# Six projections in one closing chain of Strassen products, in a hybrid decoder layer on one core

## The chip, the core and the metric

The kernel runs on one core of one Trainium2 chip. A core has a matrix engine (PE, with its weight loads listed apart as PEld), a vector engine (DVE), a scalar engine (ACT), GpSimd (POOL) and a queue engine (SP) that issues every DMA of this kernel. The metric is the device time of one execution in microseconds (us), lower is better. The kernel before takes 2838.16 us, the median of 3 runs from 2836.1 to 2838.73.

## The reference

One decoder layer over 512 tokens of width 2048: sliding-window attention with sinks, a gated DeltaNet branch, and a gated merge of the two. Everything is float32. Cut to what the change touches:

```python
proj = h @ w_in                      # 512 x 2048 times 2048 x 21056
aq, ak, av, ag, d_qkv, dz, db, da, mg_a, mg_b = split(proj)
a_out = swa_attention(rope(norm(aq)), rope(norm(ak)), av, sinks) * silu(ag)
y_a = a_out @ w_o_swa                # 2048 x 2048
o = gated_delta_rule(q, k, v, g, beta)          # 32 heads, 128 wide
o = rms_norm(o, dn_norm_w) * silu(dz)           # dz: the output gate, 4096 wide
y_b = o @ w_o_dn                     # 4096 x 2048
y = sigmoid(mg_a) * y_a + sigmoid(mg_b) * y_b   # mg_a, mg_b: the merge gates, 2048 wide each
return x + gate * (y @ w_out)        # 2048 x 2048
```

## The kernel before, in words

**Products.** Each float32 operand is cut into a high part (`hi`, fp32r) and a rest (`lo`); `split` does it with a cast on ACT (L61) and a subtraction on DVE (L62). `mm3` then issues three matmuls of 128x512 (L273, L274, L275: high by high, high by low, low by high). A *channel tile* (`channel_tile`) makes 128 channels for all 512 tokens: 16 steps of 128 along the contraction, so 48 matmuls, with the weights stationary and the token matrix `hh`/`hl` moving. Its weights are one load of 1 MB (`raw`, L215), split in two halves of 1024 columns. There are 174 channel tiles. The other way is a Strassen product (the Winograd form, `PRODUCTS`): tokens, contraction and columns are each cut in two, seven products of sums take the place of eight of quarters, and per 2048x2048 matrix there are 2 column parts x 7 = 14 products of 48 matmuls, where channel tiles need 16 x 48. In a product the token form is stationary and the weights move; a half of 1024 columns feeds 12 matmuls per product step instead of 24. Four of the seven products use sums of weight quarters. `weight_sums` forms these ahead: for one matrix 8 blocks, each with four loads of 512 KB (L1241), four additions of 128x1024 on DVE (L1246) and four stores (L1248).

**Stages.** `startup` (norm, adaLN, first tiles), `delta_keys` (16 key tiles for DeltaNet, with merge-gate tiles `mb` between them), `attention` (2 key, 16 query and 16 gate tiles, then seven merge-gate tiles `ma`), `delta_heads` (16 groups of two heads; each has the tiles q, v, v, z, z and a chain `scan` over four chunks of 128 tokens), `branch_b` (the two halves of `w_o_dn`, by Strassen, 28 products), `finish` (16 channel tiles `os` for `w_o_swa`, merged with the gates) and `output` (`w_out`, by Strassen, 14 products).

**What sets the order.** Work between matmuls is written as generators; `pump` is called once in 6 matmuls and steps them. `go` starts one that counts its waits in pumps, `paced` one that costs a budget per pump (the triangular `solve_all` at 0.36, `weight_sums` at 2.0), and `behind` ties an instruction after the latest matmul. A scheduler then fixes one order per engine; each engine and the SP queue run theirs in order. Weight loads take turns in two buffers (`wraw`), split halves in three (`whl`), so DVE can be at most three halves ahead of PE.

The steps that the prediction names: in `scan`, `pp` (L971) gives `r` on DVE (L974), then `pv` (L981), `vn` on ACT (L983), `vs` on DVE (L988), `pod` (L996 to L1000), `osb` and its squares on ACT (L1001, L1004), the new state `S` on DVE (L1011); after the last chunk a reciprocal root (`rsqrt`), the scaling of `osb` (L1030), a transposition `pto` and a product with the gate (L1037).

## Time and profile before

| | |
|---|---|
| median of 3 runs | 2838.16 us |
| the profiled execution, its span | 2839.0 us |
| PE busy | 2806.5 us (99%), 14152 matmul records |
| DVE busy | 1944.8 us (69%) |
| ACT busy | 1207.1 us (43%) |
| moved by DMA | 603.25 MB, mean 212 GB/s, queue q1 at 62.1% of 16 engines |
| vector and scalar work on one weight half | 1235 ns (L62) and 1050 ns (L61), 516 times |

A page of the profile gives busy time per engine, 40 slices of the span with the busy share in tenths, the DMA queues, the chain of waits followed back from the end, and groups of instructions by line with their mean and what ended the idle time before them. Matmuls overlap in the records, so their mean duration is longer than their spacing. The profiled execution's span is 0.8 us over the median of the runs; nothing lies around it that the runs would add.

### The profile page before, as it was taken

The numbers are of one execution on the slowest core, as the hardware profiler recorded it, in microseconds if no ns is written. First come the engines' busy times: TensorE is split into PE (matmuls) and PEld (weight loads), VectorE is DVE, ScalarE is ACT, GpSimd is POOL, SyncE is SP. The second block draws the span as 40 slices with busy tenths as digits, with TensorE's granted clock in tenths as the row PEclk, the third lists the DMA queues.
The fourth block names the chain that finished last, engine by engine and source line by source line (L and its number), as shares of the span: only waits on it lengthen the run. The fifth ranks groups of instructions, "written<-read, shape, count | busy, mean of one in ns | idle before, by whom it ended". The sixth has DMA issues, their size and how long they took to land.

```text
span 2839.0 us, 38354 instructions
## 1 busy us (share of the span) xinstructions
PE 2806.5 (99%) x14152; PEld 2283.3 (80%) x14152; DVE 1944.8 (69%) x3185; ACT 1207.1 (43%) x2476; POOL 146.0 (5%) x124
## 2 busy tenths in 40 slices
PE   8999999999999999999999999999999999999999
...
DVE  7866876867758667778766666666656766664676
...
GB/s 402 335 246 230 257 218 139 110 91 91 82 135 119 101 168 110 117 201 219 247 255 262 235 224 242 210 239 238 231 167 252 289 314 240 302 273 180 242 318 168
DMA packets 228512, 603.25 MB, mean 212 GB/s; under 512 B 76354, under 2 KB 102594, under 8 KB 188002
## 3 DMA queue, kind: packets, MB, share of 16 engines
q1 hardware_dynamic: 228324, 600.80, 62.1%
...
## 4 chain that ended last, share of the span: by engine, by line
PE 91%; DMA 3%; DVE 3%; ACT 1%; issue 1%; SPq 0%; POOL 0%; DVEq 0%; ACTq 0%; POOLq 0%
PE mm L273 22%; PE mm L275 21%; PE mm L274 21%; PE m L274 5%; PE m L273 5%; PE m L275 5%; PE pod L1000 1%; PE O L1514 1%; PE pv L981 1%; DVE wlo L62 1%; PE pod L999 1%; PE pod L996 1%; PE pp L971 1%; PE S L1451 1%; DMA wa<-in_w_ada_ss 1%
## 5 line engine op out<-in xcount | busy, mean ns | idle before, releaser
L273 PE MATMUL mm<-hh,whi 128*128 128x512 f32 x2784 | 1130.4, 406 | 1.5 <-ACT hh L61 1.5
L275 PE MATMUL mm<-hh,wlo 128*128 128x512 f32 x2784 | 1090.4, 392 | 0.0
L274 PE MATMUL mm<-hl,whi 128*128 128x512 f32 x2784 | 1087.9, 391 | 0.0
L62 DVE TENSOR_TENSOR wlo<-raw,whi 128x1024 fp32r<-128x1024 f32 x516 | 636.9, 1235 | 426.4 <-ACT whi L61 415.4
L61 ACT CAST whi<-raw 128x1024 fp32r<-128x1024 f32 x516 | 541.3, 1050 | 799.9 <-PE mm L274 566.6
L273 PEld LDWEIGHTS mm<-hh,whi 128*128 128x128 f32 x2784 | 524.0, 188 | 117.0 <-issue 14.3
L275 PEld LDWEIGHTS mm<-hh,wlo 128*128 128x128 f32 x2784 | 523.0, 188 | 113.8 <-issue 0.2
L274 PEld LDWEIGHTS mm<-hl,whi 128*128 128x128 f32 x2784 | 524.7, 188 | 100.9 <-issue 1.6
L1246 DVE TENSOR_TENSOR q<-q,q 128x1024 f32<-128x1024 f32 x96 | 124.8, 1300 | 0.0
L794 ACT ACTIVATE E<-E,neg_g 128x128 f32<-128x128 f32 x256 | 81.2, 393 | 92.3 <-POOL E L788 89.6
L831 DVE TENSOR_TENSOR A<-A,atmp 128x62 f32<-128x62 f32 (+30 forms) x124 | 109.5, 883 | 0.6
L823 DVE TENSOR_TENSOR atmp<-A 128x62 f32<-128x62 f32 (+30 forms) x124 | 107.4, 866 | 0.4
L928 POOL TENSOR_TENSOR qe<-qe,yq 128x512 f32<-128x512 f32 x32 | 54.1, 1708 | 923.9 <-DMA qe<-eg_rows 695.9
L1001 ACT COPY osb<-pod 128x256 f32<-128x256 f32 x64 | 23.8, 372 | 152.6 <-PE pod L1000 152.6
L788 POOL TENSOR_SCALAR_AFFINE_SELECT E<-E 128x512 f32<-128x512 f32 x64 | 59.1, 936 | 431.2 <-DMA E<-g_rows 384.5
L983 ACT COPY vn<-pv 128x256 f32<-128x256 f32 x64 | 23.8, 372 | 124.4 <-PE pv L981 124.4
L652 DVE SCALAR_TENSOR_TENSOR yv<-mm,convh,yv 128x511 f32<-128x511 f32 (+2 forms) x96 | 71.2, 742 | 1.1
L988 DVE TENSOR_SCALAR vs<-vn,kd 128x128 f32<-128x128 f32 x96 | 23.1, 283 | 58.3 <-ACT vn L983 58.3
L1482 ACT ACTIVATE sm<-sm,mx,rs 128x128 f32<-128x128 f32 x128 | 61.5, 482 | 3.4 <-DVE mx L1477 2.3
L1011 DVE SCALAR_TENSOR_TENSOR S<-S,egl,pod 128x128 f32<-128x128 f32 x64 | 19.3, 342 | 51.0 <-ACT junk L1004 51.0
L472 DVE SCALAR_TENSOR_TENSOR wa<-wa,silu_cb 128x2048 f32<-128x2048 f32 x22 | 50.1, 2285 | 4.8 <-DMA wa<-in_w_ada_ss 4.8
L657 ACT ACTIVATE th<-yv 128x512 f32<-128x512 f32 x32 | 20.1, 630 | 76.4 <-DVE yv L652 73.7
...
## 6 DMA issues: line engine op xcount, KB each, us to landing
...
```

The lines of the kernel that those rows point to most:

```text
L61: h = self.nc.scalar.copy(out=hi, in_=src)
L62: l = self.nc.vector.tensor_tensor(out=lo, in0=src, in1=hi.bitcast(F32), op=ALU.subtract)
L273: nc.tensor.matmul(ps, lhsT=wh, rhs=xh, start=first, stop=False)
L274: nc.tensor.matmul(ps, lhsT=wh, rhs=xl, start=False, stop=False)
L275: self.last_mm = nc.tensor.matmul(ps, lhsT=wl, rhs=xh, start=False, stop=last)
L652: nc.vector.scalar_tensor_tensor(out=y[:, s:], in0=ps[:, : T - s], scalar=w[:, j : j + 1], in1=y[:, s:], op0=ALU.mult, op1=ALU.add)
L788: self.last_mask = self.nc.gpsimd.affine_select(out=E, in_=E, pattern=[[0, NTB], [1, P]], compare_op=ALU.is_ge, fill=NEG, base=0, channel_ ...
L794: self.nc.scalar.activation(E[:, c, :], E[:, c, :], AF.Exp, bias=self.neg_g[:, c, h : h + 1])
L823: eng.tensor_tensor(out=t, in0=A[:, m : m + 1, m + 1 :].to_broadcast([P, m, n]), in1=A[:, :m, m : m + 1].to_broadcast([P, m, n]), op=ALU.mult,
L831: self.behind(eng.tensor_tensor(out=A[:, :m, m + 1 :], in0=A[:, :m, m + 1 :], in1=t, op=ALU.add))
L1246: self.behind(nc.vector.tensor_tensor(out=q[f], in0=q[x], in1=q[y], op=ALU.add))
L1482: nc.scalar.activation(t, t, AF.Exp, scale=r[:, h : h + 1], bias=mx[:, h : h + 1], accum_out=den[:, h : h + 1])
```

## The change

Three more matrices, the two merge gates (`ga`, `gb`) and `w_o_swa` (`os`), are multiplied by Strassen products. They and the two halves of `w_o_dn` (`d0`, `d1`) and `w_out` (`out`) form one chain `tail` of 84 products. The gate products use the token matrix `hh`/`hl` itself for three of their forms and make the other four from it (`h_forms`); the gates are stored by tokens (`gate_t`), so that the merge happens by tokens when a product of `os`, `d0` or `d1` is evicted; `d1`'s results are transposed in PSUM and become the forms of `out` (`out_forms`). Eight gate products come first (`EARLY`), two of them at the end of `delta_heads`.

The channel tiles that stood between keys and in attention, `mb` and `ma`, go. Output-gate tiles `z` take their places: 18 in `delta_keys`, 7 in `attention`, 7 stay in `delta_heads` (`ZHEADS`). A `z` tile is now activated, stored to DRAM (`z_d`) and read back by `scan`, so `heads` has three or four tiles per group instead of five. Weight sums are formed for six matrices instead of three: `ga`'s in `delta_keys`, `gb`'s in `attention` with additions of 128x512, the other four in `delta_heads` from group 0 on (before: from group 3). In `scan`, `vs` moves from DVE to ACT, as does a copy `Y`. The third weight buffer exists for the whole tail; `out` had five and has three.

By count, PE has 12504 instructions instead of 12792: 288 fewer of 128x512 and nothing else. DVE has 3400 instead of 3163, among them 159 more of 128x1024; ACT 2254 instead of 2081, among them 95 more casts of 128x1024; SP issues 1782 DMAs instead of 1370.

**PE, the last head group and the tail behind it.** `mm` and `m` are the big products, the others the last steps of `scan`. Before:

```order
L981 MATMUL pv<-r,tt_9106 128x128
L981 MATMUL pv<-r,tt_9108 128x128
L273 MATMUL mm<-hh,whi 128x512
...
L999 MATMUL pod<-S,qe 128x128
L1000 MATMUL pod<-vn,E 128x128
L273 MATMUL mm<-hh,whi 128x512
...
L275 MATMUL mm<-hh,wlo 128x512
L320 MATMUL pto<-ident,osb 128x128 x4
```

Between the last `pod` and `pto` 36 big matmuls stand there. With the change:

```order
L957 MATMUL pp<-S,kT 128x256
L266 MATMUL m_17720<-wlo,hh 128x512
L267 MATMUL m_17720<-whi,hl 128x512
L265 MATMUL m_17720<-whi,hh 128x512
L967 MATMUL pv<-r,tt_9523 128x128
...
L984 MATMUL pod<-vn,E 128x128
L265 MATMUL m_17720<-whi,hh 128x512
L266 MATMUL m_17720<-wlo,hh 128x512
L267 MATMUL m_17720<-whi,hl 128x512
L314 MATMUL pto<-ident,osb 128x128 x8
L265 MATMUL m_17721<-whi,hh 128x512
```

Three big matmuls stand between `pp` and `pv`, and three between the last `pod` and `pto`.

**DVE at the start of attention.** `wlo` is the split of a weight half, `kms`, `arky`, `arkt` the reciprocal root of the attention keys, `ang` and `turns` the rotary angles, `atmp` and `A` the solve, `q` a weight sum. Before:

```order
L62 TENSOR_TENSOR wlo<-raw,whi 128x1024
L73 TENSOR_TENSOR arkt<-arkt,kms 128x512
L831 TENSOR_TENSOR A<-A,atmp 128x30x33
L74 SCALAR_TENSOR_TENSOR arky<-arkt,arky 128x512
L72 SCALAR_TENSOR_TENSOR arkt<-arky 128x512
...
L823 TENSOR_TENSOR atmp<-A 128x992
L1367 TENSOR_TENSOR ak<-ak,arky 128x512
L62 TENSOR_TENSOR wlo<-raw,whi 128x1024
```

Eight instructions stand between the two splits. With the change:

```order
L69 TENSOR_TENSOR wlo<-raw,whi 128x1024
L1516 TENSOR_SCALAR ang<-ang 128x512
L1524 TENSOR_SCALAR sin<-sin,sgn 128x512
...
L1612 TENSOR_SCALAR kms<-kss 128x512
L76 TENSOR_SCALAR arky<-kms 128x512
L79 SCALAR_TENSOR_TENSOR arkt<-arky 128x512
L819 TENSOR_TENSOR atmp<-A 128x992
...
L1490 TENSOR_TENSOR q_4988<-q_4988,q_4990 128x512
...
L1540 TENSOR_TENSOR ak<-ak,partner_4683 128x512
L69 TENSOR_TENSOR wlo<-raw,whi 128x1024
```

Now 38 stand between two splits: 8 on the angles, 22 of both key roots, 4 that scale and rotate a key, 3 of the solve and one sum.

**DVE in the first head groups.** Here `r` and `S` are the steps of `scan`, `q` the sums. Before:

```order
L62 TENSOR_TENSOR wlo<-raw,whi 128x1024
L831 TENSOR_TENSOR A<-A,atmp 128x49x14
L1246 TENSOR_TENSOR q_11387<-q_11387,q_11396 128x1024
L1011 SCALAR_TENSOR_TENSOR S<-S,egl,pod 128x128 x2
...
L1246 TENSOR_TENSOR q_11396<-q_11396,q_11398 128x1024
L659 SCALAR_TENSOR_TENSOR yq<-th,yq 128x512
L831 TENSOR_TENSOR A<-A,atmp 128x50x13
L62 TENSOR_TENSOR wlo<-raw,whi 128x1024
```

With the change:

```order
L69 TENSOR_TENSOR wlo<-raw,whi 128x1024
L80 TENSOR_TENSOR rot<-rot,ms 128x8
...
L1490 TENSOR_TENSOR q_10797<-q_10797,q_10799 128x1024
L1490 TENSOR_TENSOR q_10799<-q_10799,q_10801 128x1024
L992 COPY S<-pod 128x256
L1490 TENSOR_TENSOR q_10801<-q_10797,q_10801 128x1024
L819 TENSOR_TENSOR atmp<-A 128x962
L1490 TENSOR_TENSOR q_10823<-q_10801,q_10823 128x1024
L960 SCALAR_TENSOR_TENSOR r<-pp,neg_eg,vt 128x128 x2
L69 TENSOR_TENSOR wlo<-raw,whi 128x1024
```

All four sums of a block, two or one between two splits before, stand between the same two splits, 26 instructions apart, and the next two splits follow each other closely.

The diff, cut to its core (`...` marks what is left out):

```diff
+GEMMS = ["ga", "gb", "os", "d0", "d1", "out"]
+YS = ["s1", "a12", "s2", "a22", "s4"]
+EARLY = [(e, n, m) for e in range(2) for n in range(2) for m in (0, 3)]
+ZKEYS = 18
+ZATT = 7
+ZHEADS = {2 * g + 1 for g in (1, 3, 5, 8, 10, 12, 15)}
+ZAHEAD = [h for h in range(32) if h not in ZHEADS]
...
+        z = [("z", h) for h in ZAHEAD[NFIRST:ZKEYS]]
         first = [("k", g) for g in range(NST, 8)]
-        turns = [x for g in range(8, KH) for x in (("k", g), ("mb", g - 8 + NFIRST))]
-        return first + turns + [("mb", j) for j in range(8 + NFIRST, KT)]
+        turns = [x for g in range(8, KH) for x in (("k", g), z[g - 8])]
+        return first + turns + z[KH - 8 :]
+    def items(self):
+        rest = [(e, n, m) for e in range(6) for n in range(2) for m in range(7)]
+        return EARLY + [i for i in rest if i not in EARLY]
...
+                wi(f"v{h}", 32 + h)
+            if 2 * g + 1 in ZHEADS:
+                z(2 * g + 1)
+        self.tail0 = len(jobs)
+        for e, n, m in self.items():
+            _, _, q, f = PRODUCTS[m]
+            for i in range(2):
+                src = a["w_q"][e, 2 * q[0] + n, 2 * q[1] + i] if q else self.s_d[e][n, f, i]
+                jobs.append((f"{GEMMS[e]}{n}_{m}_{i}", src))
...
+            third = j >= self.tail0 + 6 and (j - self.tail0) % 3 == 0
+            pool, tag = (self.oraw, "rawo") if third else (self.wraw, "raw")
...
+    def z_tile(self, h):
+        self.go(self.z_gate(h, self.channel_tile(f"z{h}")), 0)
+    def z_gate(self, h, ps):
+        nc = self.nc
+        pool, tag = self.zpool
+        th = pool.tile([P, T], F32, tag=tag, name="zth", bufs=1)
+        nc.scalar.activation(th, ps, AF.Tanh, scale=0.5)
+        yield 1
+        nc.vector.scalar_tensor_tensor(out=th, in0=th, scalar=1.0, in1=ps, op0=ALU.add, op1=ALU.mult)
+        yield 2
+        nc.sync.dma_start(out=self.z_d[h], in_=th)
...
+            ws = sa.enter_context(tc.tile_pool(name="wsumk", bufs=1, reuse_waits="tile"))
+            sums = self.paced(self.weight_sums(ws, [0]), 1.7)
             for kind, j in self.mixed():
                 if kind == "k":
                     self.go(self.keys(wk, j, self.channel_tile(f"k{j}")), 0)
                 else:
-                    self.merge_gate("mb", j, self.mb_d)
-            for j in range(2):
-                self.merge_gate("ma", j, self.ma_d)
+                    self.z_tile(j)
             self.drain("gate")
+            self.drain_slow(sums)
...
+            se = ExitStack()
+            ws = se.enter_context(tc.tile_pool(name="wsum", bufs=1, reuse_waits="tile"))
+            sums = self.paced(self.weight_sums(ws, range(2, 6)), 3.3)
             for g in range(KH):
-                if g == 3:
-                    sums = self.paced(self.weight_sums(ws), 2.0)
                 if g == 8:
                     self.drain_slow(self.solves)
                 self.heads(wk, g)
-            for j in range(9, 12):
-                self.merge_gate("ma", j, self.ma_d)
+            self.drain_slow(sums)
+            se.close()
+            gk = sb.enter_context(tc.tile_pool(name="gk", bufs=2, reuse_waits="tile"))
+            keep = {}
+            for e, n, m in EARLY[:2]:
+                form = PRODUCTS[m][1]
+                ps = self.product(e, n, m, self.raw_form(form))
+                self.go(self.early_evict(gk, e, n, m, ps, keep), 1)
             self.drain_live()
...
+        if 2 * g + 1 in ZHEADS:
+            self.z_tile(2 * g + 1)
...
-            nc.scalar.copy(out=vn, in_=pv)
-            yield 1
             if c < NTB - 1:
                 vs = wk.tile([P, 2, P], F32, tag="vs", name="vs", bufs=1)
                 for e in range(2):
-                    nc.vector.tensor_scalar(
-                        out=vs[:, e, :], in0=vn[:, e, :], scalar1=self.kd[:, c, 2 * g + e : 2 * g + e + 1],
-                        scalar2=None, op0=ALU.mult,
+                    nc.scalar.activation(
+                        vs[:, e, :], pv[:, e, :], AF.Copy, scale=self.kd[:, c, 2 * g + e : 2 * g + e + 1]
                     )
-            yield 1
+            nc.scalar.copy(out=vn, in_=pv)
+            yield 2
...
+        z = []
+        for e in range(2):
+            zt = wk.tile([P, T], F32, tag="z", name="zt", bufs=2)
+            nc.sync.dma_start(out=zt, in_=self.z_d[2 * g + e])
+            z.append(zt)
...
+    def raw_form(self, form):
+        k, t = {"a11": (0, 0), "a12": (8, 0), "a22": (8, 256)}[form]
+        return tuple(x[:, k : k + 8, t : t + 256] for x in (self.hh, self.hl))
+    def product(self, e, n, m, form, steps=None):
+        name = PRODUCTS[m][0]
+        ps = []
+        for t in range(2):
+            if name == "m7":
+                ps.append(self.pmb.tile([P, T], F32, tag=f"y{t}", name=name, bufs=1))
+            else:
+                ps.append(self.product_bank(name))
+        ah, al = form
+        for p in range(4):
+            hi, lo = self.half(f"{GEMMS[e]}{n}_{m}_{p // 2}")
+            for t in range(2):
+                for k in range(2):
+                    kt, cols, tsl = 2 * p + k, slice(k * T, k * T + T), slice(t * P, (t + 1) * P)
+                    self.mm3(ps[t], (ah[:, kt, tsl], al[:, kt, tsl]), (hi[:, cols], lo[:, cols]), kt == 0, kt == 7)
+                if t:
+                    self.half_done()
+                self.pump()
+                if steps and next(steps[0], True):
+                    steps.pop(0)
+        return ps
...
+        self.go(self.h_forms(A[0]), 1)
+        order = self.items()[2:]
...
+        builds = {(0, 1, 1): (2, {"a11": 4}), (2, 0, 0): (3, {"a11": 8, "s3": 3}), (3, 0, 0): (4, {"a11": 6, "s3": 7})}
+        build = {}
...
+        for e, n, m in order:
+            name, form = PRODUCTS[m][:2]
...
+            if (e, n, m) in builds:
+                to, direct = builds[e, n, m]
+                A[to].update((x, f[i]) for x, i in direct.items())
+                build[to] = self.paced(self.make_forms(to, dict(A[to])), 1.1)
...
+            lds = {}
+            if 2 <= e < 5 and name in ("m2", "m6", "m4", "m3"):
+                self.go(self.evict_loads(e, n, name, lds), 5)
+            ps = self.product(e, n, m, A[e][form], steps if e == 5 else None)
...
+            if e == 4 and m == 0:
+                ys = {}
+                self.go(self.out_forms(n, ys, A[5]), 1)
+            self.go(self.evict(wk, e, n, name, dict(done), keep, lds, ys), 1)
...
+    def h_forms(self, to):
+        nc = self.nc
+        for kt in range(8):
+            r = []
+            for k in (kt, kt + 8):
+                t = self.fo("hr")
+                nc.vector.tensor_tensor(
+                    out=t, in0=self.hh[:, k, :].bitcast(F32), in1=self.hl[:, k, :].bitcast(F32), op=ALU.add
+                )
+                r.append(t)
+            yield 2
+            yield from self.combine(kt, *r, to, 1)
...
             if name == "m2":
+                o = w("c11")
+                TT(out=o, in0=b[t], in1=k1[t], op=ALU.add)
+            elif name == "m6":
+                o = w("c22")
+                TT(out=o, in0=b[t], in1=k1[t], op=ALU.add)
+                TT(out=k1[t], in0=ps["m7", t], in1=o, op=ALU.add)
+                TT(out=k5[t], in0=o, in1=k5[t], op=ALU.add)
+                TT(out=o, in0=ps["m7", t], in1=k5[t], op=ALU.add)
+            elif name == "m4":
+                o = k1[t]
...
+        for t, o in enumerate(out):
+            if e < 2:
+                nc.scalar.activation(o, o, AF.Tanh, scale=0.5)
+            else:
+                STT(out=o, in0=lds["th", t0 + t], scalar=1.0, in1=o, op0=ALU.add, op1=ALU.mult)
+            if e > 2:
+                TT(out=o, in0=o, in1=lds["prev", t0 + t], op=ALU.add)
+            yield 1
+        for t, o in enumerate(out):
+            if e < 4:
+                dst = self.gate_t[e] if e < 2 else self.ya_d if e == 2 else self.yo_d
+                self.behind(nc.sync.dma_start(out=dst[2 * c + n, t0 + t], in_=o))
+                continue
+            pt = self.pmb.tile([P, T], F32, tag="tp", name="pty", bufs=2)
+            self.transpose4(pt, lambda j: o[:, j * P : (j + 1) * P])
+            ys[c, t0 + t] = pt
+            yield 1
...
+    def weight_sums(self, wk, which, width=1024):
...
+        for e in which:
+            w, dst = a["w_q"][e], self.s_d[e]
...
+    def sums_of(self, wk, w, dst, n, i, cols):
...
+        for k in range(3 if narrow else 4):
+            load(k)
+            yield 1.0
...
+        for f, (x, y) in enumerate(((0, 1), (1, 2), (0, 2), (2, 3))):
+            if f == 3 and narrow:
+                load(3)
+                yield 8.0
+            self.behind(nc.vector.tensor_tensor(out=q[f], in0=q[x], in1=q[y], op=ALU.add))
+            yield 4.5
+            self.behind(nc.sync.dma_start(out=dst[n, f, i][:, cols], in_=q[f]))
+        yield 7.0
...
+            self.zpool = (wk, "th")
+            ws = es.enter_context(tc.tile_pool(name="wsuma", bufs=1, reuse_waits="tile"))
+            sums = self.paced(self.weight_sums(ws, [1], 512), 2.3)
             for t in range(2):
                 self.go(self.key_pair(wk, t, self.channel_tile(f"ak{t}"), blk, kw, kd), 0)
             for n in range(4):
                 self.group(wk, kd[n], n, blk, mask, sink, qw)
-            for j in range(2, 9):
-                self.merge_gate("ma", j, self.ma_d)
+            for h in ZAHEAD[ZKEYS:]:
+                self.z_tile(h)
             self.drain_live()
+            self.drain_slow(sums)
```

726 lines of the change are left out of this document (312 added, 414 removed), and 8 rows, old and new, of the table loads.

## The prediction

> **What bounds the kernel now.** I read the page first: busy time by engine, the slices, the chain of waits.
>
> ```profile
> span 2839.0 us, 38354 instructions
> PE 2806.5 (99%) x14152; PEld 2283.3 (80%) x14152; DVE 1944.8 (69%) x3185; ACT 1207.1 (43%) x2476; POOL 146.0 (5%) x124
> ...
> PE   8999999999999999999999999999999999999999
> ...
> DVE  7866876867758667778766666666656766664676
> ...
> GB/s 402 335 246 230 257 218 139 110 91 91 82 135 119 101 168 110 117 201 219 247 255 262 235 224 242 210 239 238 231 167 252 289 314 240 302 273 180 242 318 168
> ...
> PE 91%; DMA 3%; DVE 3%; ACT 1%; issue 1%; SPq 0%; POOL 0%; DVEq 0%; ACTq 0%; POOLq 0%
> ```
>
> PE is busy 99% of the span and in every slice but the first; 91% of the chain that ended last is PE. DVE is at 69% in the mean, at 70 to 80% in many slices, and no slice is full. So the time is PE's list of instructions, and a change gains what it takes off that list, minus what PE then waits. The mean duration of a big matmul record is no price, since records overlap. The spacing is read from the timeline of PE in a head group:
>
> ```profile
> 2065.70 0.39 PE L273 MATMUL mm<-hh,whi 128*128 128x512 f32 x1
> ...
> 2072.95 0.39 PE L275 MATMUL mm<-hh,wlo 128*128 128x512 f32 x1
> ```
>
> There are 33 big matmuls from the first row to the last, 32 steps in 7.25 us: 0.2266 us each. A channel tile or a Strassen product of 48 costs 10.9 us. Next I read the span in stretches of 71 us and by stage: per row the length, then busy time and records of PE, PEld, DVE, ACT, POOL, then granted clock, DMA share, GB/s.
>
> ```profile
> 0.00:71.00 71.00, 58.46 (x380) 43.27 (x381) 53.43 (x91) 40.03 (x66) 0.21 (x4) 0.95 0.98 402
> 284.00:355.00 71.00, 71.00 (x337) 59.10 (x336) 59.13 (x97) 34.15 (x87) 7.05 (x8) 1.00 0.75 258
> 1207.00:1278.00 71.00, 68.63 (x352) 56.98 (x346) 52.90 (x81) 26.48 (x63) 4.98 (x4) 0.98 0.60 200
> 1278.00:1349.00 71.00, 70.79 (x386) 58.92 (x385) 58.16 (x93) 27.05 (x63) 4.28 (x4) 1.00 0.66 221
> 1491.00:1562.00 71.00, 71.00 (x376) 59.32 (x375) 44.37 (x74) 29.75 (x72) 7.65 (x6) 1.00 0.78 261
> 2201.00:2272.00 71.00, 69.73 (x306) 57.09 (x305) 52.62 (x73) 33.23 (x42) 0.00 (x0) 1.00 0.86 294
> 2272.00:2343.00 71.00, 71.00 (x313) 58.45 (x312) 49.32 (x57) 36.79 (x41) 0.00 (x0) 1.00 0.86 314
> 2485.00:2556.00 71.00, 69.49 (x317) 56.45 (x316) 46.37 (x65) 21.77 (x28) 0.00 (x0) 1.00 0.82 269
> 2556.00:2627.00 71.00, 71.00 (x315) 58.80 (x314) 33.60 (x53) 20.78 (x31) 0.00 (x0) 1.00 0.56 184
> 2698.00:2769.00 71.00, 71.00 (x315) 58.83 (x314) 49.52 (x56) 29.10 (x29) 0.00 (x0) 1.00 0.88 318
> ...
> 284.00:497.00 213.00, 213.00 (x985) 175.70 (x984) 158.45 (x234) 92.42 (x201) 13.77 (x16) 1.00 0.60 204
> 497.00:1036.00 539.00, 536.64 (x2812) 410.46 (x2811) 387.35 (x775) 229.73 (x521) 34.80 (x24) 1.00 0.34 109
> 1036.00:2137.00 1101.00, 1095.88 (x5770) 913.52 (x5769) 732.03 (x1187) 427.60 (x997) 82.54 (x62) 1.00 0.64 212
> ```
>
> What to see: channel tiles (2556) and Strassen products (2272) have almost the same number of PE records, 315 and 313 in 71 us, so one product costs what one tile costs. PE loses nothing beside a DVE of 59 us in 71 (284) or a DMA at 318 GB/s (2698). It loses 2.4 us at 1207, in the head groups with solve and sums, 1.3 at 2201 and 1.5 at 2485, at seams of the closing stages.
>
> **Part 1: fewer matmuls, −65.** Three matrices go from 16 tiles to 14 products each, 6 x 48 = 288 matmuls, and the instruction counts differ by just this. 288 x 0.2266 = 65.3 us. From the record counts it would be 288 x 71/315 = 64.9, or, if a few per cent of records are missing, about 63: bounds −63 to −65. The clock is 1.00 in the rows that matter, so no part of the spacing is a slow clock. By the Trainium skill, "TensorE: Matmul & The Clock Gate", section "Back-to-back issue gap", a sustained stream at N=512 runs at about 131 ns per matmul and the isolated gap is about 216; by the first the gain would be 38 us, by the second 62. The trace has 227 and decides, against the 131.
>
> The rest is what vector work PE meets with a shorter list.
>
> ```profile
> L62 DVE TENSOR_TENSOR wlo<-raw,whi 128x1024 fp32r<-128x1024 f32 x516 | 636.9, 1235 | 426.4 <-ACT whi L61 415.4 <-DMA ta_d<-atmp 5.7 <-PE pkk L760 4.3
> L1246 DVE TENSOR_TENSOR q<-q,q 128x1024 f32<-128x1024 f32 x96 | 124.8, 1300 | 0.0
> L73 DVE TENSOR_TENSOR arkt<-arkt,kms 128x512 f32<-128x512 f32 x6 | 4.1, 686 | 0.1
> L823 DVE TENSOR_TENSOR atmp<-A 128x62 f32<-128x62 f32 (+30 forms) x124 | 107.4, 866 | 0.4
> L866 DVE SCALAR_TENSOR_TENSOR zh<-zth,zh 128x512 f32<-128x512 f32 x32 | 22.0, 686 | 8.2 <-ACT zth L864 8.2
> L988 DVE TENSOR_SCALAR vs<-vn,kd 128x128 f32<-128x128 f32 x96 | 23.1, 283 | 58.3 <-ACT vn L983 58.3
> L983 ACT COPY vn<-pv 128x256 f32<-128x256 f32 x64 | 23.8, 372 | 124.4 <-PE pv L981 124.4
> L974 DVE SCALAR_TENSOR_TENSOR r<-pp,neg_eg,vt 128x128 f32<-128x128 f32 x96 | 29.3, 345 | 24.1 <-PE pp L971 23.8
> ...
> L1270 DVE TENSOR_SCALAR turns<-ang x4: 419/426/428, 471.8 to 478.8; 128x512 f32<-128x512 f32 x4
> ...
> L1558 DVE SCALAR_TENSOR_TENSOR yq<-yq x8: 415/416/421, 2609.4 to 2685.5; 128x256 f32<-128x256 f32 x8
> ```
>
> The last two rows give the price of narrower forms: 0.43 us for one operand of 128x512, 0.42 for two of 128x256.
>
> **Part 2: keys, +2.** Between 284 and 497 DVE is busy 158.5 of 213 us (74%). `ga`'s 32 sums cost 32 x 1.30 = 41.6 us over some 317 us of the stage, 28 of them here; ten of the new `z` products (0.69 each, the price of L866) add 7. DVE comes to 193 of 213, 91%; in the slice from 284 it would be 59.1 + 9.3 + 2.5 = 71 of 71. The cover is the split halves: DVE may be three ahead, 3 x 24 x 0.2266 = 16.3 us of matmuls. Nearest row below: that slice at 83% with no loss, 0. Above: 1.8% of 317 us, the mean loss of the slices at 1207 and 1278, 6. I take 2. `gb`'s half sums (64 x 0.69 = 44 us in attention's 539, where DVE has 387) fit by the mean; the start does not:
>
> **Part 3: start of attention, +10.** The order shows 38 DVE instructions between two weight splits, where there were 8. By rows: 18 steps of both key roots at 0.686 (L73's form; L72 and L74 alike) = 12.4; four more of these roots, of one operand, about 2.2; eight on the angles, six at 0.43 and two at 0.69, 4; four on keys about 3.5; three of the solve at about 1.2 for 128x992 (the 0.87 of L823 is over all its widths) = 3.5; one half sum 0.7. Together 26 us, the next split 1.2. Three halves cover 16.3 us, so PE stands 11 us if the cover is full and has nothing else; what small matmuls of attention lie there shorten it. Before, the angles were done in the keys' quiet end, and the same roots came with splits between. Bounds: 0, if other PE work fills it, and 16, if one half is missing. I take 10. Late then are the casts of the next loads, which catch up in the rest of attention, where DVE has 387 of 539 us.
>
> **Part 4: head groups, +7.**
>
> ```profile
> L649 ACT ACTIVATE yq<-mm,convh x16: 676/682/683, 1042.4 to 2052.8; 128x512 f32<-128x512 f32 x16
> ```
>
> One `yq` is made per group: (2052.8 − 1042.4)/15 = 67.4 us a group, 54.5 of it five tiles, 12.9 small matmuls. Now 16 groups have 16 + 32 + 7 = 55 tiles, 3.44 a group: 37.5 + 12.9 = 50.4 us, 806 us in all instead of 1078. DVE per group: 732/1101 x 67.4 = 44.8; minus 1.56 tiles of two splits 3.9, minus 25/16 `z` products 1.1, minus six `vs` 1.4, minus the copy `Y` 0.4, plus 2 more sums a group 2.6: 40.6 of 50.4 us, 81%, against 66% before. The solve ends in group 8 as before, so the first half lies above this mean, the second below. The sums also come in a heap: four of a block (5.2 us) inside 26 instructions between two splits. ACT gains six scalings of `vs` at about 0.28 to 0.37 a group and is at 39%, so it hides them; but they now stand ahead of `vn`, for which `pod` waits, with 12 or 6 big matmuls (1.4 us or more) as cover. The rows at 75 and 82% lose 2.4 and 0.2 us in 71, 1.8% in the mean; I put it on the first eight groups, 403 us: 7. Bounds: 0 (the slices that lose nothing), and 2.37/71 = 3.3% of 806, 27.
>
> **Part 5: from heads to tail, +7.** The last reduction of a head is on the path now. In a group before, from its last `pod` to the scaled `osb`:
>
> ```profile
> 2064.35 0.39 PE L1000 MATMUL pod<-vn,E 128*128 128x128 f32 x2
> 2064.77 0.37 ACT L1001 COPY osb<-pod 128x256 f32<-128x256 f32 x1 [3.26 <-PE pod L1000]
> 2069.11 1.28 DVE L1030 TENSOR_TENSOR osb<-osb,roy 128x512 f32<-128x512 f32 x2
> ```
>
> `pod` ends at 2064.74, the two scalings end at 2070.39: 5.65 us. At the end 36 big matmuls (8.2 us) lay under it; now 3 (0.7) do: 5.0. The last `pp` to `pv` has 3 matmuls over two steps `r` of 0.34 each and their semaphores, the last `vn` (0.37) 2: about 1. The second half of PSUM comes free only after the gate products: 1. Bounds 4 (only the first scaling awaited) and 16 (each of these steps behind a weight split and a form on DVE).
>
> **Part 6: tail, +5.** Six early products after the seam give 65.4 us. DVE has in it `h_forms`, 8 x (2 x 0.69 + 8 x 0.42) = 38, splits 24 x 1.235 = 30, evictions about 4: 72. A half covers only 12 matmuls here, so three cover 8 us, and 6 of excess can just reach PE: 4. The transfers of `d0` with its forms, gates and earlier results come to about 366 GB/s by my estimate (28 weight loads of 1 MB, 48 tiles of 256 KB for gates, earlier and new results, some 13.6 MB of forms: 55.6 MB in 152 us), where the row at 2698 carries 318 at 0.88 share, 361 when full: 1. Bounds 0 and 20. Against this, two seams of before go (2201 and 2485): −2.8. The third weight buffer, the narrower pools and the transposition in PSUM are put at nothing, hidden by 10.9 us a product.
>
> **Sum.** 2839.0 − 65.3 + 2 + 10 + 7 + 7 + 5 − 2.8 = 2801.9. The profiled execution is 0.8 us over the median, less than the bounds, so I say **2802**.
>
> **Rivals.** *The gain is kept nearly whole*: all the covers hold, the seam costs its 4: 2771 to 2786. For it: the row at 284 loses nothing at 83%. Against: the order's bursts of 26 and 38. *DVE sets the pace*: keys, attention, heads, seam and tail all near their upper ends, 6 + 16 + 27 + 16 + 20 = 85: 2856, or 2830 to 2850 when not all do. For: the heap of sums. Against: DVE's mean stays under 92% in every stage.
>
> *The queue decides, slower*: in the head groups 212 GB/s x 67.4 us = 14.3 MB a group before; now 1.6 MB fewer weights, 2.1 more for sums and 0.6 for `z`, 15.4 MB in 50.4 us, 305 GB/s, 246 MB in all. If the many small packets of these groups (broadcasts) hold it to what its fullest slice moved, 261 GB/s at 1491, then 246/0.261 = 942 us instead of 806: +136 in place of Part 4's 7, 2801.9 − 7 + 136 = 2931. It turns slower than before when the heads lose over 44 us, below 246/0.850 = 289 GB/s. Against: that slice had a share of 0.78, so 335 when full; the closing stages move 314 to 318, the first slice 402. SP issues 412 DMAs more in one queue, weights behind sums. By the Trainium skill, "DMA: Bandwidth & Descriptors", section "Bandwidth", a core alone reaches about 425 GB/s; the trace agrees with 402 at share 0.98, and by that the heads would not be held. That the change does not remove what it says is excluded by the counts.
>
> **Numbers.** Forecast 0.62, gain nearly whole 0.14, DVE 0.13, queue 0.10, anything else 0.01. 0.2% is about what a measurement can tell: 2833 to 2844. Of the DVE case half lies there, a fifth below, the rest above; with the queue, slower 0.14, same 0.09, faster 0.77. The forecast's own range is 2785 to 2820. The range wanted takes the DVE case in and most of the whole gain: 2774 to 2846, which leaves out the queue and little on either side.
>
> **What would show it.** Right: 12504 matmuls at 0.227; PE idle some 10 us near 500 us behind `wlo`, 5 to 8 us ahead of `pto` where the heads end, some us on `wlo` in the first eight groups; DVE near 80% in the heads, about 305 GB/s there with no wait of `whi` on `raw`. Wrong: `whi` waiting on `raw` from DRAM in the heads (the queue), a DVE without idle time over many groups (its pace), or a spacing other than 0.227 where the weights move and the tokens stand still, over the three times longer tail.

## The result, and the profile after

| | before | after |
|---|---|---|
| median of the runs, us | 2838.44 (2836.1 to 2839.58) | 2933.22 (2931.01 to 2936.3) |
| ratio to before, 95% interval | | 1.0335 [1.032, 1.0349] |
| span of the profiled execution, us | 2839.0 | 2933.1 |
| matmuls | 14152 | 13864 |
| moved by DMA, MB | 603.25 | 776.31 |

The change makes the kernel 95 us slower. The forecast was 36 us faster and is off by 131 us. The page of the kernel after, its first two parts and the chain of waits, shows where to look:

```profile
span 2933.1 us, 38848 instructions
PE 2812.4 (96%) x13864; PEld 2249.2 (77%) x13864; DVE 2205.7 (75%) x3422; ACT 1316.4 (45%) x2647; POOL 151.3 (5%) x124
...
PEclk9999999999999999999998999999999999999999
DMA  9889888464455548888868888866788989998875
GB/s 402 323 289 315 292 272 299 123 200 135 163 185 163 179 164 311 300 302 282 314 202 286 279 301 309 282 230 208 239 313 281 326 313 337 339 332 275 288 244 188
...
PE 77%; DVE 10%; DMA 6%; ACT 3%; issue 3%; SPq 1%; POOL 0%; DVEq 0%; ACTq 0%; POOLq 0%
```

PE now idles 121 us of the span (33 before), although its list is 288 matmuls shorter; and its busy time did not fall: 2812 us against 2806. The chain, 91% PE before, is 77% PE with 10% DVE and 6% DMA. In before the DMA row reads

```profile
DMA  9877764322243253356777667677647886885684
```

The new one is at 8 or 9 tenths, with one 6 among them, in slices 3 to 7 and 16 to 26, where before it was at 3 to 7: the keys and the heads. By stage, in the stretch view (length, then busy time and records of PE, PEld, DVE, ACT, POOL, granted clock, DMA share, GB/s): the keys without the first 71 us and the head groups from the first `yq` to the last, of before,

```profile
71.00:504.00 433.00, 428.63 (x2151) 350.69 (x2150) 315.01 (x514) 217.33 (x518) 28.45 (x34) 1.00 0.69 236
1042.00:2053.00 1011.00, 1005.88 (x5305) 838.20 (x5304) 683.28 (x1096) 397.63 (x928) 78.91 (x59) 1.00 0.65 215
```

and the same two of after, with two slices of the keys and the tail:

```profile
71.00:553.00 482.00, 449.11 (x2190) 362.53 (x2188) 372.62 (x573) 214.27 (x517) 29.89 (x34) 0.97 0.84 290
213.00:284.00 71.00, 68.12 (x330) 56.12 (x329) 49.05 (x96) 38.75 (x114) 8.25 (x8) 0.98 0.99 318
284.00:355.00 71.00, 59.99 (x255) 47.59 (x254) 54.69 (x79) 24.67 (x59) 3.93 (x4) 0.90 0.82 269
1095.00:1906.00 811.00, 766.08 (x4079) 625.38 (x4078) 611.90 (x929) 338.38 (x908) 83.31 (x60) 0.97 0.85 288
1995.00:2933.00 938.00, 921.09 (x3987) 745.24 (x3985) 695.95 (x886) 456.16 (x540) 0.00 (x0) 0.99 0.82 286
```

In the keys and in the heads the stage carries about 290 GB/s at a DMA share near .85, PE idles 33 and 45 us, and the granted clock falls to 0.97. In the heads PE's busy time is 28 us longer than in the same groups without sums (738.0, the first experiment). That second loss follows the first. The timeline of PE after one stall in the keys (start, length, instruction, and in brackets the idle time before it) shows how:

```profile
341.75 0.79 PE L267 MATMUL mm<-hh,wlo 128*128 128x512 f32 x1 [3.70 <-DVE wlo L69]
342.34 0.63 PE L265 MATMUL mm<-hh,whi 128*128 128x512 f32 x1
342.76 0.63 PE L266 MATMUL mm<-hl,whi 128*128 128x512 f32 x1
...
345.73 0.39 PE L267 MATMUL mm<-hh,wlo 128*128 128x512 f32 x1
345.96 0.39 PE L265 MATMUL mm<-hh,whi 128*128 128x512 f32 x1
```

After 3.7 us without work the matmuls follow each other by 0.43 us for 4 us, and only then by 0.23 again: the stall costs nearly 2 us more in slow matmuls, which the page books as PE being busy. The Trainium skill, "TensorE: Matmul & The Clock Gate", section "Part 1: The HAM clock gate", says that an idle window of about 3.4 us halves the clock until a window of work has passed; the trace agrees, 0.43 against 0.23 for 4 us.

What PE waits for in the heads, by the view of waits (total us, times, longest):

```profile
PE mm L267 <- DVE wlo L69: 16.2, 9, 6.0
PE mm L265 <- ACT whi L68: 15.0, 9, 3.6
PE pod L980 <- ACT vs L972: 5.2, 6, 1.7
```

18 waits for halves of weights, two thirds of all idle time there. Before a half can be split, its cast `whi` on ACT needs the load, and the forecast had named a `whi` that waits on `raw` as the sign of the queue. It is there, in ACT's waits of the same stretch:

```profile
ACT whi L68 <- DMA raw<-in_w_ch: 18.2, 8, 6.9
```

The sum of the differences to the forecast, from the marks of the stages (first `kss`, first and last `yq`), all of the profiled executions:

| stage | before | forecast | after | off by |
|---|---|---|---|---|
| start and keys | 503.9 | 515.9 | 553.0 | +37 |
| attention | 538.6 | 538.6 | 541.9 | +3 |
| heads, first to last `yq` | 1010.3 | 756 | 811.4 | +55 |
| last group, seam and tail | 786.2 | 991 | 1026.9 | +35 |
| span | 2839.0 | 2801.9 | 2933.1 | +131 |

(The forecast's column is before, with its parts put where they fall: 12 us in the keys; in the heads 51 tiles instead of 75 between the two marks, so 1010.3 less 24 x 10.9, plus 7; the last row is what is left of 2801.9. Up to the last start of `pto` the last group takes 89.4 us before and 89.2 after, the tail behind it 696.8 and 937.7.)

### The profile page after: what moved, and what is told of

Read it like the earlier page. It is cut to its first block, busy times and chain, and to the rows that moved or that the text cites. A ratio compares the mean times of both kernels' runs of the same rounds, so it can differ in the third digit from the quotient of the medians.

```text
span 2933.1 us, 38848 instructions
## 1 busy us (share of the span) xinstructions
PE 2812.4 (96%) x13864; PEld 2249.2 (77%) x13864; DVE 2205.7 (75%) x3422; ACT 1316.4 (45%) x2647; POOL 151.3 (5%) x124
## 2 busy tenths in 40 slices
DMA packets 286565, 776.31 MB, mean 265 GB/s; under 512 B 82946, under 2 KB 107138, under 8 KB 241314
## 4 chain that ended last, share of the span: by engine, by line
PE 77%; DVE 10%; DMA 6%; ACT 3%; issue 3%; SPq 1%; POOL 0%; DVEq 0%; ACTq 0%; POOLq 0%
PE mm L267 13%; PE mm L265 13%; PE mm L266 13%; PE m L266 9%; PE m L267 9%; PE m L265 9%; DVE wlo L69 2%; DMA q<-in_w_q 1%; DMA s_d<-q 1%; DVE q L1490 1%; ACT whi L68 1%; PE pod L984 1%; PE pv L967 1%; PE O L1761 1%; PE pp L957 1%
## 5 line engine op out<-in xcount | busy, mean ns | idle before, releaser
L69 DVE TENSOR_TENSOR wlo<-raw,whi 128x1024 fp32r<-128x1024 f32 x588 | 722.7, 1235 | 327.8 <-ACT whi L68 326.2
L265 PE MATMUL mm<-hh,whi 128*128 128x512 f32 x2016 | 825.5, 409 | 24.7 <-ACT whi L68 24.3
L267 PE MATMUL mm<-hh,wlo 128*128 128x512 f32 x2016 | 803.9, 399 | 26.1 <-DVE wlo L69 26.0
L266 PE MATMUL mm<-hl,whi 128*128 128x512 f32 x2016 | 798.2, 396 | 0.0
L265 PEld LDWEIGHTS mm<-hh,whi 128*128 128x128 f32 x2016 | 384.4, 191 | 115.5 <-ACT whi L68 28.2
L267 PEld LDWEIGHTS mm<-hh,wlo 128*128 128x128 f32 x2016 | 383.6, 190 | 116.4 <-DVE wlo L69 34.4
L266 PEld LDWEIGHTS mm<-hl,whi 128*128 128x128 f32 x2016 | 384.4, 191 | 73.9 <-issue 1.5
L1490 DVE TENSOR_TENSOR q<-q,q 128x1024 f32<-128x1024 f32 (+1 forms) x224 | 244.3, 1091 | 16.3 <-DMA q<-in_w_q 14.9
L642 DVE SCALAR_TENSOR_TENSOR yv<-mm,convh,yv 128x511 f32<-128x511 f32 (+2 forms) x96 | 71.4, 743 | 19.7 <-ACT yv L639 18.9
L266 PE MATMUL m<-wlo,hh 128*128 128x512 f32 x192 | 76.9, 401 | 3.8 <-DVE wlo L69 3.8
L265 PE MATMUL m<-whi,hh 128*128 128x512 f32 x192 | 77.6, 406 | 2.0 <-ACT whi L68 1.8
```

Of the source, the lines that this page charges most:

```text
L69: l = self.nc.vector.tensor_tensor(out=lo, in0=src, in1=hi.bitcast(F32), op=ALU.subtract)
L265: nc.tensor.matmul(ps, lhsT=wh, rhs=xh, start=first, stop=False)
L266: nc.tensor.matmul(ps, lhsT=wh, rhs=xl, start=False, stop=False)
L267: self.last_mm = nc.tensor.matmul(ps, lhsT=wl, rhs=xh, start=False, stop=last)
L642: nc.vector.scalar_tensor_tensor(out=y[:, s:], in0=ps[:, : T - s], scalar=w[:, j : j + 1], in1=y[:, s:], op0=ALU.mult, op1=ALU.add)
L1490: self.behind(nc.vector.tensor_tensor(out=q[f], in0=q[x], in1=q[y], op=ALU.add))
```

## The experiments

**Sums or not, and which half of them.** One kernel does without the sums of weights, one does their transfers without the additions.

```diff
 # no_sums
-        for e in which:
+        for e in ():
-  ... else self.s_d[e][n, f, i]
+  ... else a["w_q"][e, 2 * (f // 2) + n, 2 * (f % 2) + i]
 # no_adds
-            self.behind(nc.vector.tensor_tensor(out=q[f], in0=q[x], in1=q[y], op=ALU.add))
```

> The changed kernel without any weight sum: no loads of quarters, no additions, no stores; where a product would read a stored sum it reads a quarter of the same matrix, as many bytes, so the output is not the reference's. Theory A (the additions in the vector engine's order keep weight splits back) and theory B (the sums' transfers hold up the weight loads) both expect 2785 to 2815 us: the stages keys and heads lose their 49 and 55 us almost whole. Theory C (fewer big matmuls stand over chains of the same length: it is the shape of the stages, not the sums) expects 2880 us or more.

> The changed kernel with the loads of quarters and the stores of the sums kept, but the 224 additions left out, so a quarter is stored in place of each sum. Theory A expects the time of the kernel without sums within 15 us; theory B expects 2900 us or more, since all bytes still move; theory C 2880 or more.

2816.06 us, 0.9917 [0.9902, 0.9932], without sums, which leaves theory C (2880 or more) out; 2917.06, 1.0271 [1.0256, 1.0286], with their transfers alone. The heads, first `yq` to last, of the one and of the other:

```profile
1052.00:1790.00 738.00, 738.00 (x4116) 615.28 (x4115) 471.14 (x811) 341.77 (x904) 74.07 (x58) 1.00 0.46 144
```

```profile
1089.00:1888.00 799.00, 762.77 (x4079) 623.94 (x4078) 461.92 (x804) 337.55 (x909) 70.78 (x60) 0.98 0.86 298
```

Without sums PE is busy all of 738 us: this is what the shortened groups cost with nothing in their way, and after loses 811.4 − 737.7 = 73.7 us on it. With the transfers and no addition DVE has less to do than without sums (462 against 471), and 61.7 us are lost all the same. So the additions are worth 16 us of the whole kernel, and the transfers the rest of the 117 us between after and no sums. In the keys it is alike: 553.0 us with sums, 556.8 with transfers alone, 521.0 with neither.

**Fewer scalings on ACT, additions elsewhere.** Two tries at the pace of an engine: the scalings of `vs` and the copy `Y` go back to DVE; the additions go to GpSimd.

```diff
 # vs_dve
-        nc.scalar.copy(out=Y, in_=py)
+        nc.vector.tensor_copy(out=Y, in_=py)
 ...
-                    nc.scalar.activation(
+                    nc.vector.tensor_scalar(
 # sums_pool
-            self.behind(nc.vector.tensor_tensor(out=q[f], in0=q[x], in1=q[y], op=ALU.add))
+            self.behind(nc.gpsimd.tensor_tensor(out=q[f], in0=q[x], in1=q[y], op=ALU.add))
```

> The changed kernel with the scaled vs and the copy Y back on the vector engine, in the order before (vn first). If the scalar engine's queue is what the heads wait for (vs and vn behind weight casts), the heads gain 15 us or more: below 2918 us. Theory A expects 2930 to 2950 us, since the vector engine gets about 35 us more; theory B expects no change within 6 us.

> The changed kernel with all weight additions on GpSimd. Theory A expects 2800 to 2860 us if the two engines do not slow each other, and a smaller gain if GpSimd's additions make the vector engine's instructions longer, as some 128x512 products beside GpSimd are (0.69 us grows to 1.8 us at times). Theory B expects 2915 us or more.

The first changes nothing that matters: 2929.28, 1.0309 [1.0287, 1.0331]. The second is far worse, 3070.52, 1.0804 [1.0765, 1.0844]. Groups of instructions by line in it (count, busy us, mean ns, idle before), of GpSimd and then of DVE,

```profile
L1490 POOL TENSOR_TENSOR q<-q,q 128x1024 f32<-128x1024 f32 x160 | 426.6, 2666 | 479.4 <-DMA q<-in_w_q 433.5 <-issue 24.8 <-DMA zt<-z_d 10.7
```

```profile
L69 DVE TENSOR_TENSOR wlo<-raw,whi 128x1024 fp32r<-128x1024 f32 x588 | 790.6, 1352 | 372.8 <-ACT whi L68 369.8 <-DMA raw<-s_d 1.6
```

and of after:

```profile
L69 DVE TENSOR_TENSOR wlo<-raw,whi 128x1024 fp32r<-128x1024 f32 x588 | 722.7, 1235 | 327.8 <-ACT whi L68 326.2 <-DMA ao_d<-sg 0.2
L1490 DVE TENSOR_TENSOR q<-q,q 128x1024 f32<-128x1024 f32 x160 | 200.5, 1253 | 4.6 <-DMA q<-in_w_q 3.5
```

An addition takes 2666 ns there instead of 1253, and each of DVE's 588 splits, 1352 instead of 1235. The Trainium skill, "SBUF — State Buffer", section "🔬 SBUF: two separate sides", has a DVE operation with two SBUF inputs and a GpSimd operation that reads SBUF shut each other out; this trace agrees in direction, the splits are 9% longer. GpSimd itself waits for the sums' loads (433.5 of its 479.4 idle us), so this run does not show what additions taken off DVE are worth; the kernel without additions does.

**Bytes, transfers, queue.** Four kernels: half the bytes of each sum with the same number of instructions; twice the number of transfers with the same bytes; the sums' transfers issued by GpSimd instead of SP; the sums of `os` in attention instead of the heads.

```diff
 # half_bytes (load; addition and store alike)
-  dma_start(out=t, in_=w[2 * c + n, 2 * r + i][:, cols])
+  dma_start(out=t[:, : width // 2], in_=w[2 * c + n, 2 * r + i][:, cols.start : cols.start + width // 2])
 # double_count (load; store alike)
+            for u in range(2):
+                ... dma_start(out=t[:, u * hw : (u + 1) * hw], in_=...)
 # pool_queue (load; store alike)
-            self.behind(nc.sync.dma_start(out=t, in_=...))
+            self.behind(nc.gpsimd.dma_start(out=t, in_=...))
 # move_os
-            sums = self.paced(self.weight_sums(ws, range(2, 6)), 3.3)
+            sums = self.paced(self.weight_sums(ws, range(3, 6)), 2.5)
-            sums = self.paced(self.weight_sums(ws, [1], 512), 2.3)
+            sums = self.paced(self.weight_sums(ws, [1, 2], 512), 4.6)
```

> The changed kernel with every load and store of the weight sums at half the columns: the same number of transfers, half their bytes, and additions half as wide; where a product would read a stored sum it reads a quarter of the same size, so the output is not the reference's. Theory B1 (the rate of the sums' bytes beside the stage's other transfers) expects at least two thirds of the 117 us that the kernel without sums regained, since the heads then need 305 - 62 = about 240 GB/s: 2835 to 2860 us. Theory B2 (the number of transfers, each issued in order on one queue) expects less than a third: 2895 us or more.

> The changed kernel with each load and store of the sums cut into two transfers of half the columns: the same bytes, twice the number. B1 expects 2925 to 2950 us (rows of 2 KB in place of 4 KB may cost some rate). B2 expects a loss of the size of the one to be explained, 2990 us or more.

> The changed kernel with the sums' loads and stores issued by GpSimd in place of the queue engine, so that weight loads do not stand behind a store that waits for an addition. B2, in the form that the queue's order holds the weight loads up, expects 2880 us or less. B1 expects 2920 us or more.

> The changed kernel with one of the heads' four matrices of sums (w_o_swa's) formed in attention beside the gate's, in half widths at twice the budget. Attention moved 109 to 185 GB/s, the heads 280 to 317. B1 expects the heads to regain 20 to 40 us and attention to lose less than 15: 2895 to 2925 us in all. If the vector engine's list decides, attention loses 40 us or more with its 64 further additions, and the whole is 2940 us or more.

| kernel | median, us | ratio | heads, us |
|---|---|---|---|
| after | 2933.22 | 1.0335 [1.032, 1.0349] | 811.4 |
| half_bytes | 2829.01 | 0.9958 [0.9941, 0.9974] | 742.3 |
| double_count | 2939.59 | 1.0341 [1.0322, 1.036] | 813.7 |
| pool_queue | 2925.36 | 1.0296 [1.0281, 1.0311] | 799.8 |
| move_os | 2930.78 | 1.032 [1.0305, 1.0336] | 747.7 |

The heads of the first and of the last of these four:

```profile
1061.00:1804.00 743.00, 740.31 (x4121) 616.21 (x4120) 543.98 (x939) 342.68 (x913) 73.39 (x60) 1.00 0.74 233
```

```profile
1159.00:1906.00 747.00, 740.75 (x4115) 614.73 (x4114) 576.93 (x906) 343.31 (x911) 81.98 (x60) 1.00 0.83 276
```

It is bytes. Half of them give back 69 of the 74 us in the heads and 28 of 49 in the keys; their number, doubled, costs the heads 2 us; another issuing engine gives 12. The Trainium skill, "DMA: Bandwidth & Descriptors", section "Issuing engines are not separate DMA queues", says that another issuer saves only the time of issuing. The 12 us are as little as that would give, but `pool_queue` is no clean test of it. PE waits there for no weight half any more; its 40 idle us in the heads are steps of `scan`, above all `pu` behind `Y` (18.1 us) and `pod` behind `vs` (14.4). ACT's `E` waits 71.4 us for GpSimd, which now issues the transfers (2.8 in after). One wait went and another came.

Moving one matrix out takes the heads to 276 GB/s and gives back 64 us there, more than the 20 to 40 expected; but attention pays 57 (598.8 instead of 541.9), where less than 15 was expected, and start and keys 7. In attention the rate is no answer:

```profile
560.00:1159.00 599.00, 556.65 (x2762) 416.32 (x2763) 453.88 (x895) 227.24 (x512) 32.85 (x22) 0.95 0.63 201
```

At 201 GB/s PE is idle 42 us, 19.9 of it behind `sm` on DVE, and DVE stands 63.3 us for the loads of its additions, 64 more than in after. So sums cost time here at a low rate; by these waits it is through the order of DVE's list, which no run tested.

**Is it the rate?** If transfers at such a rate are enough, the kernel before should lose time too when it is given them; if the rate per time decides, then long groups should bear more sums, and short groups none. First, before with each sum stored twice:

```diff
 # before_traffic, on the kernel before
+                            self.behind(nc.sync.dma_start(out=self.x_d[u, n, f, i][:, cols], in_=q[f]))
```

> The kernel before with one transfer more for each of its 96 sums: the sum is stored a second time, to a place that nobody reads; no vector work is added, and the output is whole. Its head groups with sums moved some 237 GB/s; 50 MB more over 853 us make it about 296, the rate at which the heads of the changed kernel (about 300) lose. If the rate beside the heads' other transfers is the cause (theory B1), the heads lengthen by 25 us or more: 2865 to 2910 us. If it is something of the changed kernel (shorter groups, its order), 2845 us or less.

2841.72, 1.0002 [0.9992, 1.0011]: no loss. The heads, and a stretch of 284 us with sums in them:

```profile
1040.00:2050.00 1010.00, 1006.43 (x5301) 836.01 (x5300) 676.11 (x1095) 396.40 (x926) 75.29 (x59) 1.00 0.77 262
1491.00:1775.00 284.00, 283.08 (x1488) 235.30 (x1488) 175.37 (x294) 110.83 (x266) 19.01 (x18) 1.00 0.86 296
```

The expectation, a loss of 25 us or more, was wrong, and not by its premise: the stage's mean is 262 GB/s only because its first three groups have no sums, and where sums run the rate is the 296 that was aimed at. At this rate and a share of .86, more than the heads of after move (288, .85), PE is busy all but 0.9 of 284 us. So a rate moved near 290 costs nothing by itself. What may cost is a need above it, and what after needs is its bytes over the time that it would take without loss: 288 GB/s x 811 us = 233.6 MB in 737.7 us, 317 GB/s. So two more kernels, made to reach that rate in other ways: before with 25 of its `z` tiles left out of the head groups and the sums begun earlier with extra stores; and after with 25 redundant `z` tiles added to its groups and extra stores of the sums.

```diff
 # before_short, on the kernel before
-        for e in range(2):
-            self.go(self.zgate(wk, self.channel_tile(f"z{2 * g + e}"), st), 0)
+        if g in ZG:
+            self.go(self.zgate(wk, self.channel_tile(f"z{2 * g + 1}"), st), 0)
-                if g == 3:
-                    sums = self.paced(self.weight_sums(ws), 2.0)
+                if g == 0:
+                    sums = self.paced(self.weight_sums(ws), 2.6)
+                            if f < 2:
+                                self.behind(nc.sync.dma_start(out=self.x_d[u, n, f, i][:, cols], in_=q[f]))
 # long_groups, on the kernel after
-        if 2 * g + 1 in ZHEADS:
-            self.z_tile(2 * g + 1)
+        for h in (2 * g, 2 * g + 1):
+            if h in ZHEADS:
+                self.z_tile(h)
+            else:
+                self.go(self.z_gate(h, self.channel_tile(f"zz{h}"), self.x2_d, "zz"), 0)
+            if f < extra:
+                self.behind(nc.sync.dma_start(out=x_d[n, f, i][:, cols], in_=q[f]))
```

> The kernel before with 25 of the 32 output-gate tiles left out of the heads (a tile of the attention's output is read in place of each, so the output is not the reference's), the sums begun in the first group at a budget of 2.6, and half of them stored a second time: groups of three or four tiles as in the changed kernel, at about 300 GB/s. Theory L expects the 15 groups, 738 us where nothing is lost, to take 780 us or more: about 2610 us in all. If it is something else of the changed kernel, 750 us or less: below 2580 us.

> The changed kernel with 25 output-gate tiles computed a second time in the heads (results stored where nobody reads), so that each group has five tiles again, with the heads' sums spread over the longer stage and three of four stored a second time, so that the rate stays near 300 GB/s. Theory L (the transfers cost time only where a group has few matmuls to stand over its chain) expects the 15 groups at 1010 to 1025 us, nothing lost: about 3145 us in all. If the rate costs the changed kernel that much whatever the groups' length, they take 1055 us or more: 3185 us or more.

2624.82 us, 0.9243 [0.9228, 0.9259], with the work left out; 3186.06, 1.1224 [1.1207, 1.1241], with the work added. The heads of the one, then of the other:

```profile
1041.00:1836.00 795.00, 760.75 (x4118) 624.19 (x4117) 601.13 (x1005) 315.68 (x811) 69.03 (x56) 0.98 0.81 284
```

```profile
1094.00:2158.00 1064.00, 1031.23 (x5303) 845.74 (x5302) 687.33 (x1025) 405.47 (x1001) 81.69 (x60) 0.99 0.86 301
```

Both lose now. With the needed rate worked out for each kernel as above (bytes of its heads over 737.7 us, or over the 1010.3 of five-tile groups; for `before_short` and `long_groups` this time without loss is an estimate, taken from another kernel):

| kernel | needed, GB/s | moved, GB/s | lost in the heads, us |
|---|---|---|---|
| no_sums | 144 | 144 | 0 |
| before | 215 | 215 | 0 |
| half_bytes | 235 | 233 | 4.6 |
| before_traffic | 262 | 262 | 0 |
| move_os | 280 | 276 | 9.9 |
| before_short | 306 | 284 | 57.4 |
| after | 317 | 288 | 73.7 |
| long_groups | 317 | 301 | 54.5 |
| no_adds | 323 | 298 | 61.7 |
| pool_queue | 323 | 298 | 62 |

Up to 280 GB/s nothing or little is lost, from 306 on 55 to 74 us, whichever kernel it is, whatever the length of its groups or its additions. And the rate moved stays at 284 to 301. With the additions gone and the rate kept the loss stays; with the additions kept at half width and the bytes halved it goes. So it is shown that the sums' bytes, in a stage this short, become time, and by means over the stage the need at which they do so lies between 280 and 306 GB/s, and in long groups above 296, by the stretch of `before_traffic`. A fixed ceiling of the transfers is not shown: two of the kernels that lose move less (after 288, `before_short` 284) than that stretch carried without loss. Nor is it shown whether the DMA engines set the limit or the order in the one queue of SP, where a weight load stands behind stores that wait; `pool_queue` was to separate the two and brought a new wait instead.

**Is it the buffers?** The share is .81 to .87 in the rows that lose over 50 us, so the engines are not quite full. A third buffer for raw weights in the heads, and a second set for the sums:

```diff
 # raw3
+            if self.heads0 + 2 <= j < self.tail0 - 3 and (j - self.heads0) % 3 == 2:
+                pool, tag = self.hraw, "rawh"
-        vt = wk.tile([P, NTB, P], F32, tag="vt", name="vt", bufs=4)
+        vt = wk.tile([P, NTB, P], F32, tag="vt", name="vt", bufs=3)
 # two_sets
-            sums = self.paced(self.weight_sums(ws, range(2, 6)), 3.3)
+            sums = self.paced(self.two_sets(ws, range(2, 6)), 3.3)
+                t = wk.tile([P, 512], F32, tag=f"q{k}", name=f"q{k}", bufs=2)
```

> The changed kernel with a third 1 MB buffer for weights in the heads, so that a load may take a tile's time longer before PE waits. If the loads come late by their own length only (depth), the heads regain 20 us or more of their 55: below 2915 us. If the transfers as a whole do not keep up (rate), or others than the weights are late, less than 10 us: 2923 us or more.

> The changed kernel with the sums of keys and heads in two sets of half-width buffers of the same size together: the same bytes and additions, but a load is issued some 6 us of matmuls after the store that frees its buffer and a whole block ahead of its addition, so that queue and vector engine seldom wait for a sum's transfer. If these waits hold the one queue up (theory S), keys and heads regain 40 us or more of their 106: below 2893 us. If the rate itself does it (theory R), less than 15: 2918 us or more.

2931.66, 1.0322 [1.0305, 1.0339], and 2943.48, 1.0353 [1.033, 1.0377]. The third buffer gives the heads 14 us (797.1) and their last group takes 13 back (102.0 instead of 89.2). The second set gives the heads 5 (806.6) and costs the keys 9. Neither gets back more than a fifth of the 74.

**The solve.** Group 9 of after takes 87.0 us, where without sums it takes 59.4: 28 of the 74 us are lost in this one group. There the solve hands over its matrices, a burst of stores. The queue does not move more for it: from 1502 to 1589 us it moves 244 GB/s at a share of .76, and by SP's waits it stands 14.9 us until ACT has written what five of these stores take, and 24.2 for additions ahead of their stores. In `pool_queue`, where the sums' transfers stand in another queue, the group takes 66.9 us and moves 337 GB/s at a share of 1.00. This points to the order in the one queue, though no run shows it alone. A faster solve moves the burst.

```diff
 # solve_fast
-            self.solves = self.paced(self.solve_all(), 0.36)
+            self.solves = self.paced(self.solve_all(), 0.5)
```

> The changed kernel with the budget of the triangular solve raised from 0.36 to 0.5 per step, so that its second half is ready for the ninth head group well ahead. In the changed kernel that group takes 87.0 us where the kernel without sums takes 59.4. If the hand-over through memory of the second half is late there, the group loses at most 8 us: 2905 to 2915 us, unless the earlier solve delays attention by as much. If the group is slow for another reason, no change within 4 us.

2934.73, 1.0325 [1.031, 1.0341], heads 810.8. Group 9 falls to 63.5 us, and groups 3 and 4 take 25 us more. But the burst lies ahead of these now: its stores are issued from 1108 to 1173 us, in groups 1 and 2, and these two are no longer than in after (93.8 against 94.9). So the burst itself is not shown to cost time; the heads lose the same 73 us in all, with the burst in either place.

**The start of attention.** The wrapping of the angles into one turn left out, eight instructions on DVE, which makes its burst there shorter.

```diff
 # rope_short
-            for lim, cmp, by in ((math.pi, ALU.is_gt, -2 * math.pi), (-math.pi, ALU.is_lt, 2 * math.pi)):
-                nc.vector.tensor_scalar(out=n, in0=t, scalar1=lim, scalar2=by, op0=cmp, op1=ALU.mult)
-                nc.vector.tensor_tensor(out=t, in0=t, in1=n, op=ALU.add)
```

> The changed kernel with the rotary angles not wrapped into one turn (8 steps on the vector engine left out, some 4.5 us; angles and so the output are not the reference's). The key statistics wait on the scalar engine behind the cosine, and that behind these steps. If this is what PE stands for at the start of attention (a gap of 10.5 us), the stage of keys gets 4 to 8 us shorter, 2924 to 2930 us in all; if the sums' transfers hold it, no change within 3 us.

2922.62, 1.0287 [1.0269, 1.0304], a little below the range expected. Start and keys take 543.7 instead of 553.0 us. The timeline of after at that place shows why:

```profile
551.81 0.63 ACT L1527 ACTIVATE cos<-ang 128x512 f32<-128x512 f32 x1 [3.72 <-DVE ang L1516]
552.34 0.58 ACT L1605 ACTIVATE ksq<-mm 128x512 f32<-128x512 f32 x1
...
552.98 2.08 PE L1610 MATMUL kss<-ksq,blk 128*128 128x512 f32 x2 [10.09 <-ACT ksq L1605]
```

and of the shortened kernel:

```profile
543.70 1.12 PE L1607 MATMUL kss<-ksq,blk 128*128 128x512 f32 x2 [2.34 <-ACT ksq L1602]
```

PE waits 10.1 us for the key statistics, whose square `ksq` stands on ACT behind the cosine, which waits for DVE's angles; with a shorter burst it waits 2.3. Without sums it still waits 7.7 there, so the sums have little part in it.

**The spacing in the tail.** The forecast's third sign of being wrong was a spacing other than 0.227 where the weights move and the token forms stand still. The timeline of the tail of after has it. Rows 1 and 2 are the first and last of the 48 matmuls of a product on form 8, rows 3 and 4 of one on form 3:

```profile
2712.57 0.39 PE L265 MATMUL m<-whi,f8h 128*128 128x512 f32 x1
...
2723.22 0.40 PE L267 MATMUL m<-whi,f8l 128*128 128x512 f32 x1
2723.46 0.39 PE L265 MATMUL m<-whi,f3h 128*128 128x512 f32 x1
...
2734.43 0.39 PE L267 MATMUL m<-whi,f3l 128*128 128x512 f32 x1
```

10.65/47 = 0.2266 us on form 8, 10.97/47 = 0.2334 on form 3. All products on forms 0 to 4 are slow like this, none on 5 to 8; the forms' tiles differ in where they lie. Counted from the sizes of the kernel's buffers (the traces have no addresses), the forms 5 to 8 lie a multiple of 1024 bytes from the split halves of the weights, 0 to 4 a multiple plus 416. The kernel before had filling tiles named for alignment, which the change takes out. Two kernels put one back, of 96 bytes and of 416:

```diff
 # aligned
+        fm.tile([P, 24], F32, name="alignb")
 # same_place
+        fm.tile([P, 104], F32, name="alignb")
```

> The changed kernel with 96 bytes left free above three of the tail's form buffers, so that the five slots f0 to f4 begin at a multiple of 128 bytes instead of 32 bytes past a multiple of 64; nothing else moves. In the tail's trace matmuls with a stationary form in f0 to f4 follow at 0.231 to 0.238 us and those in f5 to f8, at multiples of 64, at 0.227. If the place in memory is the cause, the 2304 of them fall to about 0.227 and the tail gets 10 to 15 us shorter: 2918 to 2923 us. If it is the neighbours' traffic, nothing changes: 2930 us or more.

> The changed kernel with 416 bytes left free above three form buffers, so that all nine slots lie at a multiple of 1024 bytes from the split halves, as f5 to f8 do already (96 bytes, the run before, gave a multiple of 64 for f0 to f4 and no gain). If the distance modulo 1024 of the two operands sets the spacing, f0 to f4 fall from 0.233 to 0.227 us and the tail gets 10 to 15 us shorter: 2918 to 2923 us. If not, 2930 us or more.

2934.8, 1.0331 [1.0315, 1.0346]: nothing, with a remainder of 320 bytes. And 2918.6, 1.0268 [1.0253, 1.0284], with none: the tail takes 924.2 instead of 937.7 us. A product on form 3 in it:

```profile
2709.29 0.39 PE L265 MATMUL m<-whi,f3h 128*128 128x512 f32 x1
...
2719.94 0.39 PE L267 MATMUL m<-whi,f3l 128*128 128x512 f32 x1
```

10.65/47 = 0.2266. So the place of the standing operand against the moving one costs or saves 3% of a product. The trace of before had a sign of it: its products on a form `f0` take 10.76 us from first to last matmul (2188.59 to 2199.35), 0.2289 each.

**Together.** The second set, the faster solve and the tile of 416 bytes in one kernel, and the sums in attention begun behind the key tiles:

```diff
 # combo
+            self.solves = self.paced(self.solve_all(), 0.5)
+            sums = self.paced(self.two_sets(ws, range(2, 6)), 3.3)
+        fm.tile([P, 104], F32, name="alignb")
```

> The three edits together, and the gate's sums in attention begun only after the two key tiles, so that the rotary angles don't stand behind a sum that waits for its buffer. If S, the hand-over and the place all hold: 2840 to 2870 us, near the kernel before. If only the hand-over holds: 2890 to 2910.

2927.15, 1.0299 [1.0279, 1.0318]: neither of the two ranges expected. The tail keeps its 14 us, the heads give 9, start and keys cost 16 more. No kernel with the whole computation beats the one before.

## Why the prediction was wrong

**What bounds the kernel now** was right for before, and its conclusion, a change gains what it takes off PE's list, holds only while the transfers keep up. The view of DMA had been read for single slices and not held against the new stage lengths in more than one of them.

**Part 1, −65:** 288 matmuls went, as counted. The spacing did not hold: 2304 matmuls of the tail, on the forms 0 to 4, run at 0.2334 instead of 0.2266 in the mean, some 15 us, of which one filling tile returns 13.5. The prediction had read the spacing in a head group and taken it over for the products by counts of records (315 and 313 in 71 us). The taken-out tiles stood in the diff, and the prediction put nothing on them.

**Part 2, keys +2: the step that failed first.** It asked whether DVE has the time for the sums, and found that it has. It did not ask whether the queue has. The row of before, 236 GB/s over 433 us, is 102 MB; 64 transfers of 512 KB for the sums of `ga` make it 136 MB, 313 GB/s. The trace of after has 290 x 482 = 140 MB, 323 GB/s needed and 290 moved, and one slice at share .99 carries 318. 49 us are lost in start and keys; 32 of them go without sums, and of the 17 that stay 7.7 are the wait of Part 3.

**Part 3, start of attention +10:** the place is right, and the size, 10.1 us behind a burst on DVE. What PE waited for is another thing than said: the key statistics, held on ACT behind the cosine, not a weight split. The 10 was worked out from the splits' cover, so its size came out right in part by luck. That the wait hangs on the angles is shown by the shortened burst, which returns 9.3.

**Part 4, heads +7: the step that failed for most.** The mean of DVE and its heaps were priced, and 1.8% of the stage was put on them. The groups without sums run at 738 us, even 11 below the 749 that 24 tiles of 10.9 us fewer give, so the shortening was sound. What was lost is 74 us, and only some 12 of these hang on the additions (73.7 against 61.7 without them). The rest goes with the bytes of the sums' transfers, on which the step put nothing.

***The queue decides, slower*, chance 0.10:** in its main point this is what happened. Its need was right, 305 GB/s as estimated, 317 as measured. It was argued away by a division: 261 GB/s at a share of .78, "so 335 when full". The stage as a whole never got full. Where it lost time it stopped at a share near .85 and 284 to 301 GB/s; and a share of .99 in the keys was 318 and not 402. The 402 and the 314 to 318 came from other mixes. The section "Bandwidth" of the Trainium skill's "DMA: Bandwidth & Descriptors", which the rival names, has 425 GB/s for a core alone; its table also has 341 for single transfers of 1 MB. The head groups moved 288: the measurement decides. The rival's own sum, 2931, came out right by two errors: its ceiling of 261 was too low (the heads lost 74, not 136), and it left the keys and the tail out. That it matched 2933 is luck. "Below 289 GB/s it turns slower" was a fair mark, and after moved 288.

***DVE sets the pace*** is refuted by the kernel without additions (−16 us); ***the gain kept nearly whole*** by the result.

**Part 5, seam +7:** right in its main wait. The first transposition of the last group waits for the scaled `osb`,

```profile
1994.08 1.77 PE L314 MATMUL pto<-ident,osb 128*128 128x128 f32 x8 [4.10 <-DVE osb L1016]
```

4.1 us by this view, where 5.0 was said. The 2 beside it no run took apart, and the last group's length (89.2 us, 89.4 before) says nothing of them, since it holds other tiles now.

**Part 6, tail +5:** the tail, with the last group, is 35 us over the forecast. 13.5 are the spacing. Behind the seam PE is idle 16.9 us (the stage row); its waits there add up to 12.3, and the largest is

```profile
PE m L266 <- DVE wlo L69: 9.5, 7, 2.9
```

where the forecast had 4 for this and 1 for the transfers. No run took these waits apart. With them counted at 7 over the forecast, about 14 us of the 35 stay without a shown cause.

Open are also why the heads stop at a share near .85 rather than at 1, where neither a third weight buffer nor a second set of sums changed much; some 9 us of the keys, and whether the engines' rate or the order in SP's queue sets the limit. Which power of two the distance of the operands must be a multiple of is not settled either: by the count of the buffers, remainders of 416 and 320 bytes were slow, 0 was fast.
